# Attention with transposed rows in batches of eight key blocks, their products with V one batch behind

## The chip, the cores and the metric

The kernel runs on one core of one Trainium2 chip, in one launch. The metric is the time of that launch in microseconds (us). The kernel before has a median of 4274.78 us over three runs (4272.74 to 4277.41).

## What is computed

The reference is a trunk of two layers over 2048 tokens of width 1024, in float32. Each layer normalises x, projects it, and runs four groups of four heads (64 dims each) in parallel: A stick-breaking attention, B latent attention, C attention over 256 keys chosen by an indexer, D differential attention. The groups' outputs are gated, joined and projected back. Cut to the part that the change touches:

```python
def softmax_attention(q, k, v, scale):        # B; C and D have the same last line
    def block(i, qb, kk, vv):                 # a query tile of 128, all keys up to it
        s = einsum('bqhd,bshd->bhqs', qb, kk) * scale
        p = softmax(where(vis, s, -inf))
        return einsum('bhqs,bshd->bqhd', p, vv)
# D: w = softmax(s1) - lam * softmax(s2), then w @ v
# C: the softmax runs over the chosen keys alone
```

## The kernel before

A layer is worked off in sweeps over 16 query tiles of 128 tokens: `a` (group A and the indexer of C), `h` (latents and gates), `d0` and `d1` (group D, two heads in each), `b`, `c`, `o` (output projection). Query tile i sees nb = i + 1 key blocks of 128.

In D, B and C a tile is split into units, one per head (in C two heads at a time for i < `PAIRED` = 12). A unit has a first part and a second part.

The first part, `att_row` (L826), makes a row: scores of the tile against all keys (TensorE, L837, in PSUM tiles `s`), scaled and copied to a row `rw` in SBUF with the minimum (VectorE, L841 or L843, L846), and their exponentials in place (ScalarE, L847). Rows lie in a ring of `R2` = 30720 bytes per partition (`self.rows`); a row of tile i takes 512 (i + 1) bytes. In D two rows are joined into one with lambda (L1074).

The second part, `att_pv` (L850), multiplies a row by V. TensorE needs the row transposed, so for each group of four key blocks (two blocks of two heads in the paired units of C) it makes four transposes into one PSUM tile `tp` (L283), ScalarE or VectorE copies it to a scratch tile `pt` (L285 or L287), and TensorE multiplies by V into the PSUM tile `y` (L866), even blocks into partitions 0 to 63 and odd ones into 64 to 127. There are two buffers `tp` and three `pt`; the indexer uses `pt` as well (L495, L505). `EV` says how many of the copies go to ScalarE: 0.6 of them in C, all in D, 0.6 in B. A product is one instruction in the program and two records in the trace.

What sets the order: the parts are generators. `drive` (L1338) merges the second part of a unit with the first part of the next unit and with the projections of later tiles (L256, L257, L260) and their transposes (`pj`, L283), each taken in shares of its stated cost (`yield`). The framework then orders every engine's instructions by that priority and by its own estimate of when operands are ready, so TensorE's queue holds the pieces of several units mixed. Each engine works through its queue in order. Behind the two layers stands a branch to a general way that is not taken with these inputs; its instructions are in the built program and not in the trace.

In the rows below, PE is TensorE's matmuls and transposes and PEld its weight loads, DVE VectorE, ACT ScalarE, POOL GpSimd.

Of the kernel before, what the change touches and what calls it, by code (L numbers as in the profile page):

```python
# [18 lines left out]
PSUM = bass.MemoryType.PSUM  # L19
# [38 lines left out]
R2 = 30720  # L58


def merge(*gens):
    """Interleaves generators, whose first item is their whole cost and whose others are costs of steps."""
    act = []
    for g in gens:
        if g is None:
            continue
        tot = next(g)
        act.append([0.0, max(tot, 1.0), g])
    while act:
        a = min(act, key=lambda t: t[0] / t[1])  # L70
        try:
            a[0] += next(a[2])
        except StopIteration:
            act.remove(a)
# [15 lines left out]
class Share:  # L90
    """A generator taken in shares of its cost."""
# [16 lines left out]
class Trunk:  # L108
# [53 lines left out]
    def g2(self, shape, dtype=F32):  # L162
        """scratch of the projections, up to 2 KB"""
        return self.wk.tile(shape, dtype, name="g2", bufs=4)

    def pt(self, shape, dtype=F32):
        """scratch of the attention's inner loops, up to 2 KB"""
        return self.wk.tile(shape, dtype, name="pt", bufs=3)

    def o2(self, shape, dtype=F32):  # L170
        """scratch of the attention's results, up to 2 KB"""
        return self.wk.tile(shape, dtype, name="o2", bufs=2)
# [22 lines left out]
    def split(self, hi, lo, raw, eng="pp"):  # L195
        """hi: raw rounded, lo: what that leaves"""
        if eng[0] == "p":
            self.pcopy(hi, raw)
        else:
            self.nc.scalar.copy(hi, raw)  # L200
        if eng[1] == "p":
            self.psub(lo, raw, hi.bitcast(F32))
        else:
            self.nc.vector.tensor_sub(lo, raw, hi.bitcast(F32))  # L204

    def weights(self, W, key, src, pieces, n, kt=KT, first=False):
        """src [kt*128, cols] in DRAM; pieces (column, count) side by side make n columns."""
        nc = self.nc
        w = W[key] = ([], [], n)
        yield kt * 100.0  # L210
        for k in range(kt):
            # the very first ones come all at once, through the memory of the rows
            raw = self.rows.tile([128, n], F32, name="w_raw0") if first else self.wk.tile([128, 512], F32, name="w_raw")
            o = 0
            for c, m in pieces:
                nc.sync.dma_start(raw[:, o:o + m], src[k * 128:(k + 1) * 128, c:c + m])
                o += m
            hi = self.ring.tile([128, n], F32R, name="w_hi")
            lo = self.ring.tile([128, n], F32R, name="w_lo")
            self.split(hi, lo, raw[:, :n], "ad" if k % 3 in WAD or first and k % 3 == 0 else "pp")  # L220
            w[0].append(hi)
            w[1].append(lo)
            yield 100.0
# [4 lines left out]
    def early(self, i, n):  # L228
        """who splits: ScalarE and VectorE while the attention of tile i leaves them time, else GpSimd"""
        return "ad" if FROM <= i < n else "pp"  # L230
# [32 lines left out]
    def rstd(self, who, ss, n, width):  # L263
        """(ss / width + eps) ** -0.5 of [128, n]"""
        nc = self.nc
        r = self.wk.tile([128, 16], F32, name="rs")[:, :n]
        if who in BYACT:
            nc.scalar.activation(r, ss, AF.Ln, bias=self.eps, scale=1.0 / width)
            nc.scalar.activation(r, r, AF.Exp, scale=-0.5)
            return r  # L270
        nc.gpsimd.tensor_scalar(r, ss, 1.0 / width, EPS, op0=OP.mult, op1=OP.add)  # L271
        nc.gpsimd.tensor_tensor(r, r, self.mhalf[:, :n], op=OP.pow)  # L272
        return r

    def transposes(self, dst, srcs, eng="act", tag="pj"):
        """srcs: up to four [128, m] fp32 views; dst [m, len, 128] view."""
# [3 lines left out]
        # sources of rounded results are rounded themselves  # L280
# [3 lines left out]
        if eng == "act":  # L284
            nc.scalar.copy(dst, p[:m, :len(srcs), :])  # L285
        else:
            nc.vector.tensor_copy(dst, p[:m, :len(srcs), :])  # L287

    def piece(self, st, key, i, shape, dtype=F32):
        """the tile of key that holds token tile i, of four each; last but one dim of shape is 4 tiles long"""  # L290
# [5 lines left out]
    def at(self, offset, g):  # L296
        """generator g, its instructions scheduled as if they came offset instructions later"""
# [17 lines left out]
    def a_load(self, l, i, st):  # L315
        """x tile -> normalised, transposed, split"""
# [41 lines left out]
    def functions_a(self):  # L358
        """has ScalarE take the set of functions with both exponential and logarithm"""
        self.nc.scalar.preload_act_table_set("natural_log_exp_and_others")  # L360

    def a_first(self, l, i, st):
# [33 lines left out]
        for r in range(2):  # L396
# [6 lines left out]
            if zr is not None:  # L403
                # what is left of the stick after these blocks is at most exp(X0 - z0)
# [63 lines left out]
    def hilo64(self, u):  # L468
        """u [128, 5, 64]: [hi lo] of the first four, [hi hi] and [lo lo] of the last"""
# [9 lines left out]
    def ci_score(self, l, i, st, tied=True):  # L479
        """scores of tile i into a row buffer"""  # L480
# [3 lines left out]
        # the general search takes two more rows  # L484
# [3 lines left out]
        for c0 in range(0, n, 512):  # L488
            w = min(512, n - c0)
            # equal scores of zero rank by their index  # L490
# [25 lines left out]
    def ci_search(self, l, b):  # L516
        """per row of the tiles of b a threshold with 249..256 scores at or above it, then the 256th itself"""
# [17 lines left out]
        def count(dst, th):  # L535
            """number of scores at or above th"""
# [24 lines left out]
        # threshold among the zeros: bracket (-(n + 0.5) TINY, Z) .. (0.5 TINY, P0)  # L561
# [13 lines left out]
        # above zero  # L575
# [9 lines left out]
        # below zero  # L585
# [12 lines left out]
        for it in range(NITER):  # L598
# [16 lines left out]
            # outside the bracket: its middle  # L615
# [8 lines left out]
        # the 256th of each row: 256 - count below the threshold found  # L624
# [64 lines left out]
    def ga_att(self, l, i, st):  # L689
        """stick-breaking of query tile i over every key block"""  # L690
# [54 lines left out]
    def gc_search(self, l, i, st):  # L745
        """the 256 greatest scores of each row, equal ones by lowest index: bit by bit"""
# [14 lines left out]
        for bit in range(30, -1, -1):  # L761
# [4 lines left out]
            # from zero up: keep the bit while 256 are at or above; from zero down: while fewer are above  # L766
# [10 lines left out]
        # indices of the equal ones, 4096 for the others  # L777
# [26 lines left out]
    def flag(self):  # L804
        """0 where every check of the short ways held"""
# [20 lines left out]
    def att_row(self, i, passes, scale, mn, ls, bias=None):  # L826
        """a row of masked, scaled, negated scores and their exponentials"""
# [22 lines left out]
    def att_pv(self, i, rows, v, y, ev):  # L850
        """y[0:64 | 64:128, :] += even | odd key blocks of rows^T; rows: list of [128, n], y: [128, len * 128]"""
# [4 lines left out]
        for j0 in range(0, nb, step):  # L856
            js = range(j0, min(j0 + step, nb))
            pt = self.pt([128, 4, 128])
            self.ev += ev
            self.transposes(pt[:, :len(js) * m, :], [r[:, j * 128:(j + 1) * 128] for j in js for r in rows],  # L860
                            eng="act" if self.ev >= 1 else "dve", tag="tp")
            if self.ev >= 1:
                self.ev -= 1
            for c, j in enumerate(js):
                o = 64 * (j % 2)
                nc.tensor.matmul(y[o:o + 64, :], v(j), pt[:, c * m:(c + 1) * m, :].rearrange("p a b -> p (a b)"),  # L866
                                 start=(j < 2), stop=(j >= nb - 2), skip_group_check=True)
            yield (109.0 + 125.0) * m * len(js)

    def att_out(self, i, y, nu):  # L870
        """y [128, nu * 128] (dims of even | odd blocks, queries) -> [128 queries, nu, 64] in PSUM"""
# [9 lines left out]
    def norm_out(self, i, y, ls, col):  # L881
        """four heads' results over their sums, to columns col of scratch"""
# [129 lines left out]
    def rope_gain(self, gq, gk, d):  # L1012
        """[128, (q k), (cos sin), d]: gains as the two products of the rotation meet them"""
# [9 lines left out]
    def tables(self, i, d, g):  # L1023
        """cosines and signed sines of token tile i times the gains of q and k: [128, (q k), (cos sin), d]"""
# [8 lines left out]
    def rope(self, u, w, p, tab, nq, nk, h):  # L1033
        """u = p cos + swapped p sin of nq heads of q and nk of k, with their tables"""
# [67 lines left out]
    def lambdas(self, l):  # L1102
        """-lam and the sub-layer norm's gain times (1 - lam_init)"""
# [18 lines left out]
    def start_h(self, l, st):  # L1122
        """latents of B"""
# [36 lines left out]
    def gates(self, i, h, w, col, tag):  # L1160
        """pre-activations of the gates from column col on"""
# [22 lines left out]
    def proj_b(self, l, i, st):  # L1184
# [40 lines left out]
        # q: [hi hi] [lo lo], k: [hi lo]; rotary part q: [hi hi lo], k: [hi lo hi]  # L1225
# [19 lines left out]
    def prep_b(self, l, i, st):  # L1245
# [4 lines left out]
        # heads 0 1: hi hi lo lo, heads 2 3 the same  # L1250
# [87 lines left out]
    def drive(self, sweeps):  # L1338
        """sweeps: (start, prep, units, l, st); tiles one after another, their projections two tiles ahead"""
# [119 lines left out]
```

## Time and profile before

| what | value |
| --- | --- |
| runs, median (lowest to highest) | 4274.78 us (4272.74 to 4277.41) |
| the profiled execution, first to last instruction | 4276.6 us |
| busy: PE, PEld, DVE, ACT, POOL | 3937.6, 3249.9, 2906.3, 2371.9, 1650.7 us |
| D, layer 0 (both halves) | 670 to 1285 us of the span |
| B, layer 0 | 1285 to 1650 us |
| C, layer 0 | 1650 to 1915 us |
| D, B, C of layer 1 | 2790 to 3405, 3405 to 3770, 3770 to 4035 us |

The profiled execution's time is its span; it lies 1.8 us above the median of the runs. Matmuls are pipelined and their ends are modelled, so that two in a row can overlap in the rows: how long a piece of work holds the engine is read from one start to the next. In the list of waits, "issue" stands for idle time that nothing in the profile released.

### The profile page before, as it was taken

How to read it: one execution, taken by the hardware profiler on the slowest of the kernel's cores; microseconds unless marked ns; L12 is line 12 of the kernel's file. 1: busy time of each engine (PE TensorE's matmuls, PEld its weight loads, DVE VectorE, ACT ScalarE, POOL GpSimd, SP SyncE). 2: the span in 40 equal slices, each digit the busy share in tenths (PEclk: the TensorE clock that was granted, in tenths of full speed). 3: DMA queues.
4: the chain of work that ended last, by engine and by line, in shares of the span. 5: the costliest groups of instructions: out<-in, count | busy, mean ns of one | idle time of the engine just before them, and what ended most of it. 6: DMA issues, size and time to landing. Idle time of an engine off the chain costs nothing.

```text
span 4276.6 us, 75274 instructions
## 1 busy us (share of the span) xinstructions
PE 3937.6 (92%) x25833; PEld 3249.9 (76%) x25833; DVE 2906.3 (68%) x10326; ACT 2371.9 (55%) x4846; POOL 1650.7 (39%) x2350
## 2 busy tenths in 40 slices
PE   6999996899988999999989999979999889999999
PEld 6877786777866777777878787867788667777777
DVE  3798788787875655663337988887968766555622
ACT  3656677465665545454126667765666655554621
POOL 2333423665664433420033343337747544344100
PEclk9999997899988999999999999979999899999999
DMA  3222531121110002114522225311211100021144
GB/s 104 80 77 84 175 112 58 50 59 52 50 35 26 19 23 68 50 44 139 167 88 81 81 91 172 114 54 48 61 53 49 36 22 18 26 74 46 59 138 139
DMA packets 204842, 312.60 MB, mean 73 GB/s; under 512 B 63777, under 2 KB 147873, under 8 KB 203937
## 3 DMA queue, kind: packets, MB, share of 16 engines
q1 hardware_dynamic: 204448, 307.69, 22.7%
q8 instruction: 206, 3.38, 0.3%
q14 instruction: 188, 1.53, 0.1%
HBM read 211.89 MB, written 95.72 MB: 72 GB/s over the span
## 4 chain that ended last, share of the span: by engine, by line
PE 57%; DVE 20%; ACT 6%; POOL 6%; DMA 5%; issue 5%; SPq 0%; DVEq 0%; ACTq 0%; POOLq 0%
PE y L866 9%; PE s L837 8%; PE tp L283 7%; PE pj L256 7%; PE pj L257 6%; PE pj L260 6%; PE s L256 3%; PE s L257 3%; PE s L260 3%; ACT junk L538 2%; DVE sc L506 2%; DVE rw L843 2%; PE pj L283 2%; DMA w_raw<-w_in 2%; DVE rw L841 2%
## 5 line engine op out<-in xcount | busy, mean ns | idle before, releaser
L256 PE MATMUL pj<-w_hi,h_hi 128*128 128x384 f32 (+4 forms) x2560 | 880.2, 352 | 51.5 <-POOL w_hi L193 22.9
L257 PE MATMUL pj<-w_lo,h_hi 128*128 128x384 f32 (+4 forms) x2560 | 863.9, 345 | 8.0 <-DVE w_lo L204 4.0
L847 ACT ACTIVATE rw<-rw,at_mn 128x896 f32<-128x896 f32 (+15 forms) x512 | 615.7, 1204 | 173.1 <-DVE at_mn L846 148.2
L285 ACT COPY pt<-tp 128x512 f32<-128x512 f32 (+3 forms) x689 | 358.1, 529 | 467.8 <-PE tp L283 390.3
L256 PEld LDWEIGHTS pj<-w_hi,h_hi 128*128 128x128 f32 x2560 | 505.7, 198 | 88.9 <-POOL w_hi L193 26.0
L283 PE MATMUL tp<-ident,rw 128*128 128x128 f32 x3264 | 540.4, 287 | 34.4 <-DVE rw L1074 20.3
L257 PEld LDWEIGHTS pj<-w_lo,h_hi 128*128 128x128 f32 x2560 | 505.3, 197 | 32.4 <-DVE w_lo L204 6.6
L260 PE MATMUL pj<-w_hi,h_lo 128*128 128x384 f32 (+4 forms) x2560 | 523.4, 338 | 0.0
L283 PEld LDWEIGHTS tp<-ident,rw 128*128 128x128 f32 x3264 | 365.4, 143 | 172.2 <-issue 117.5
L843 DVE TENSOR_SCALAR_CACHE_REDUCE rw<-s 128x512 f32<-128x512 f32 x576 | 383.0, 684 | 108.2 <-PE s L837 73.7
L260 PEld LDWEIGHTS pj<-w_hi,h_lo 128*128 128x128 f32 x2560 | 434.1, 190 | 25.7 <-issue 10.8
L271 POOL TENSOR_SCALAR rs<-ss 128x2 f32<-128x2 f32 (+4 forms) x224 | 61.7, 276 | 802.8 <-DVE ss L987 202.7
L538 ACT ACTIVATE junk<-sg,st_T 128x1152 int8<-128x1152 f32 (+4 forms) x224 | 293.9, 1312 | 83.9 <-DVE st_T L622 56.9
L272 POOL TENSOR_TENSOR rs<-rs,mhalf 128x8 f32<-128x8 f32 (+5 forms) x256 | 317.0, 1239 | 16.9
L287 DVE COPY pt<-tp 128x512 f32<-128x512 f32 (+3 forms) x247 | 152.9, 619 | 197.6 <-PE tp L283 163.5
L837 PE MATMUL s<-dk,qa 96*128 96x512 f32 (+3 forms) x640 | 233.5, 424 | 43.9 <-DVE rw L843 22.3
L187 POOL TENSOR_TENSOR h_lo<-x4a,h_hi 128x1024 fp32r<-128x1024 f32 x103 | 255.5, 2480 | 39.4 <-PE pj L260 22.8
L193 POOL TENSOR_SCALAR hl<-g 128x256 fp32r<-128x256 f32 (+1 forms) x384 | 151.2, 408 | 286.9 <-DVE g L452 61.3
L837 PE MATMUL s<-bk,qa 128*128 128x512 f32 (+6 forms) x960 | 257.8, 394 | 1.2 <-DVE at_mn L841 0.7
L283 PE MATMUL pj<-identr,hl 128*128 128x128 f32 (+1 forms) x1280 | 174.6, 258 | 74.1 <-POOL hl L187 47.9
L193 POOL TENSOR_SCALAR h_hi<-x4a 128x1024 fp32r<-128x1024 f32 x103 | 115.2, 1119 | 319.8 <-PE pj L257 156.1
L841 DVE CUSTOM_DVE_ANT_0 rw<-s,maskR 128x128 f32<-128x128 f32 (+3 forms) x400 | 187.7, 478 | 56.7 <-PE s L837 55.5
(267 smaller groups left out, 8731.5 us busy)
## 6 DMA issues: line engine op xcount, KB each, us to landing
x4a<-hT SPq DMA_DIRECT2D x128, 512.0 KB, 3.5
x4a<-x SPq DMA_DIRECT2D x32, 512.0 KB, 3.5
hT<-x4a SPq DMA_DIRECT2D x32, 512.0 KB, 2.6
x4a<-y SPq DMA_DIRECT2D x32, 512.0 KB, 3.5
x4b<-gate SPq DMA_DIRECT2D x32, 512.0 KB, 3.6
x4c<-x SPq DMA_DIRECT2D x32, 512.0 KB, 4.1
y<-o SPq DMA_DIRECT2D x96, 128.0 KB, 2.1
w_raw<-w_in SPq DMA_DIRECT2D x48, 192.0 KB, 2.6
```

The costliest lines, as they stand in the source:

```text
L256: nc.tensor.matmul(p[:, :n], hi[:, k, :], whi[k], start=(k == 0), stop=False)
L257: nc.tensor.matmul(p[:, :n], hi[:, k, :], wlo[k], start=False, stop=False)
L260: nc.tensor.matmul(p[:, :n], lo[:, k, :], whi[k], start=False, stop=(k == kt - 1))
L272: nc.gpsimd.tensor_tensor(r, r, self.mhalf[:, :n], op=OP.pow)
L283: nc.tensor.transpose(p[:m, j, :].bitcast(dst.dtype), s.bitcast(dst.dtype), ident)
L285: nc.scalar.copy(dst, p[:m, :len(srcs), :])
L538: nc.scalar.activation(self.junk[:, :ns[g]], Sg[g], AF.Sign, bias=th[:, g:g + 1], scale=-1.0, accum_out=dst[:, g:g + 1])
L837: nc.tensor.matmul(p[:, :w], x, y, start=(k == 0), stop=(k == len(ops) - 1))
L841: nc.vector.tensor_tensor_reduce(o, p[:, :w], b, -scale, 3.0e38, OP.add, OP.min, m)
L843: nc.vector.tensor_scalar(o, p[:, :w], -scale, None, op0=OP.mult, op1=OP.min, accum_out=m)
L847: nc.scalar.activation(rw, rw, AF.Exp, bias=mn, scale=-1.0, accum_out=ls)
L866: nc.tensor.matmul(y[o:o + 64, :], v(j), pt[:, c * m:(c + 1) * m, :].rearrange("p a b -> p (a b)"), start=(j < 2), stop=(j >= nb - 2), ski ...
```

## The change

`att_pv` takes two groups at a time as a batch: up to eight transposes and two copies. The products of a batch are made by a new function, `pv_batch`, after the transposes of the next batch have been recorded. The first product of a batch is made to wait for the last copy of the batch. The scratch tiles `pt` get a fourth buffer, and the ring of the rows becomes 128 bytes smaller. `transposes` now returns its copy instruction. The other lines of the difference take comments out, so that lines are numbered anew: products are L880, scores L836, transposes stay L283.

```diff
-R2 = 30720
+R2 = 30592
...
     def pt(self, shape, dtype=F32):
-        return self.wk.tile(shape, dtype, name="pt", bufs=3)
+        return self.wk.tile(shape, dtype, name="pt", bufs=4)
...
         if eng == "act":
-            nc.scalar.copy(dst, p[:m, :len(srcs), :])
-        else:
-            nc.vector.tensor_copy(dst, p[:m, :len(srcs), :])
+            return nc.scalar.copy(dst, p[:m, :len(srcs), :])
+        return nc.vector.tensor_copy(dst, p[:m, :len(srcs), :])
...
     def att_pv(self, i, rows, v, y, ev):
         nc = self.nc
         nb = i + 1
         m = len(rows)
         step = 4 // m
-        for j0 in range(0, nb, step):
-            js = range(j0, min(j0 + step, nb))
-            pt = self.pt([128, 4, 128])
-            self.ev += ev
-            self.transposes(pt[:, :len(js) * m, :], [r[:, j * 128:(j + 1) * 128] for j in js for r in rows],
-                            eng="act" if self.ev >= 1 else "dve", tag="tp")
-            if self.ev >= 1:
-                self.ev -= 1
+        groups = [range(j0, min(j0 + step, nb)) for j0 in range(0, nb, step)]
+        before = None
+        for g in range(0, len(groups), 2):
+            pts = []
+            for js in groups[g:g + 2]:
+                pt = self.pt([128, 4, 128])
+                self.ev += ev
+                last = self.transposes(pt[:, :len(js) * m, :], [r[:, j * 128:(j + 1) * 128] for j in js for r in rows],
+                                       eng="act" if self.ev >= 1 else "dve", tag="tp")
+                if self.ev >= 1:
+                    self.ev -= 1
+                pts.append((js, pt))
+            yield 109.0 * m * sum(len(js) for js, _ in pts)
+            if before is not None:
+                yield self.pv_batch(before, m, nb, v, y)
+            before = pts, last
+        yield self.pv_batch(before, m, nb, v, y)
+
+    def pv_batch(self, batch, m, nb, v, y):
+
+        pts, last = batch
+        first, n = True, 0
+        for js, pt in pts:
             for c, j in enumerate(js):
                 o = 64 * (j % 2)
-                nc.tensor.matmul(y[o:o + 64, :], v(j), pt[:, c * m:(c + 1) * m, :].rearrange("p a b -> p (a b)"),
-                                 start=(j < 2), stop=(j >= nb - 2), skip_group_check=True)
-            yield (109.0 + 125.0) * m * len(js)
+                x = self.nc.tensor.matmul(y[o:o + 64, :], v(j), pt[:, c * m:(c + 1) * m, :].rearrange("p a b -> p (a b)"),
+                                          start=(j < 2), stop=(j >= nb - 2), skip_group_check=True)
+                if first:
+                    self.tc.add_manual_dep(x.ins, last.ins.name,
+                                           mybir.DependencyInfo(mybir.DependencyClass.Sync, mybir.DependencyReason.DATA),
+                                           reason="one run of products")
+                first = False
+                n += m
+        return 125.0 * n
```

How the built order changes is shown at three places; the numbers tell the buffers apart.

First, TensorE in B of layer 0, query tile 12 (13 key blocks, so groups of 4, 4, 4 and 1 blocks per head): `tp` are transposes of a row, `y` products of a `pt` with V. Before:

```order
L283 MATMUL tp_19071<-ident_199,rw_18930 128x128 x4
L837 MATMUL s_19278<-bk_17135,qa_18595 128x512 x3
L866 MATMUL y_18937<-pt_19044,bv_15295 64x128 x4
L283 MATMUL tp_19087<-ident_199,rw_18930 128x128 x4
L866 MATMUL y_18937<-pt_19070,bv_16180 64x128 x4
L283 MATMUL tp_19103<-ident_199,rw_18930 128x128
L866 MATMUL y_18937<-pt_19086,bv_17035 64x128 x4
L283 MATMUL tp_19123<-ident_199,rw_19037 128x128 x4
L866 MATMUL y_18937<-pt_19102,bv_18166 64x128
```

The same head with the change:

```order
L283 MATMUL tp_19074<-ident_199,rw_18930 128x128 x4
L283 MATMUL tp_19081<-ident_199,rw_18930 128x128
L880 MATMUL y_18937<-pt_19044,bv_15295 64x128 x4
L880 MATMUL y_18937<-pt_19051,bv_16180 64x128 x4
L836 MATMUL s_19289<-bk_17137,qa_18598 128x512 x3
L283 MATMUL tp_19123<-ident_199,rw_19037 128x128 x4
L283 MATMUL pj_18966<-identr_201,hl_18878 128x128 x2
L283 MATMUL pj_18972<-identr_201,hl_18879 128x128 x2
L283 MATMUL pj_18966<-identr_201,hl_18878 128x128 x2
L880 MATMUL y_18937<-pt_19073,bv_17036 64x128 x4
L880 MATMUL y_18937<-pt_19080,bv_18163 64x128
```

Products of two groups now follow each other, and two runs of products stand where four stood.

Second, TensorE in B of layer 0, query tile 5 (6 key blocks: one batch of 4 and 2 blocks per head). Before:

```order
L283 MATMUL tp_16877<-ident_199,rw_16773 128x128 x4
L283 MATMUL tp_16902<-ident_199,rw_16773 128x128 x2
L866 MATMUL y_16875<-pt_16876,bv_15295 64x128 x4
L283 MATMUL tp_16941<-ident_199,rw_16868 128x128 x4
L866 MATMUL y_16875<-pt_16901,bv_16180 64x128 x2
L283 MATMUL tp_16961<-ident_199,rw_16868 128x128 x2
L283 MATMUL pj_16652<-identr_201,hl_16596 128x128 x2
L866 MATMUL y_16875<-pt_16940,bv_15295 64x128 x4
```

With the change:

```order
L283 MATMUL tp_16877<-ident_199,rw_16773 128x128 x4
L283 MATMUL tp_16884<-ident_199,rw_16773 128x128 x2
L283 MATMUL tp_16941<-ident_199,rw_16868 128x128 x4
L880 MATMUL y_16875<-pt_16876,bv_15295 64x128 x4
L880 MATMUL y_16875<-pt_16883,bv_16180 64x128 x2
L283 MATMUL tp_16948<-ident_199,rw_16868 128x128 x2
L283 MATMUL pj_16652<-identr_201,hl_16592 128x128 x2
```

The first transposes of the next head (`rw_16868`) now stand ahead of the products of this head, which are one run.

Third, TensorE in the second half of D, layer 0, query tile 12, second head of the half. Before:

```order
L283 MATMUL tp_14926<-ident_199,rw_14867 128x128 x4
L866 MATMUL y_14810<-pt_14897,dv_14137 64x128
L283 MATMUL tp_14974<-ident_199,rw_14867 128x128 x4
L837 MATMUL s_14988<-dk_14289,qa_14550 128x256
L837 MATMUL s_14998<-dk_11641,qa_14550 128x512
L866 MATMUL y_14810<-pt_14925,dv_11475 64x128 x4
L283 MATMUL tp_15006<-ident_199,rw_14867 128x128 x4
L837 MATMUL s_15016<-dk_12543,qa_14550 128x512
L866 MATMUL y_14810<-pt_14973,dv_12426 64x128 x4
```

With the change:

```order
L283 MATMUL tp_14926<-ident_199,rw_14878 128x128 x4
L283 MATMUL tp_14933<-ident_199,rw_14878 128x128 x4
L836 MATMUL s_15029<-dk_13342,qa_14553 128x512
L283 MATMUL tp_14974<-ident_199,rw_14878 128x128 x4
L836 MATMUL s_15037<-dk_14292,qa_14553 128x256
L283 MATMUL tp_14981<-ident_199,rw_14878 128x128
L880 MATMUL y_14810<-pt_14925,dv_11490 64x128 x4
L880 MATMUL y_14810<-pt_14932,dv_12424 64x128 x4
L836 MATMUL s_15083<-dk_11644,qa_14553 128x512
L880 MATMUL y_14810<-pt_14973,dv_13204 64x128 x4
```

All transposes of the head now stand ahead of its first product.

## Rows read from the trace of the kernel before

**Rows 1.** The page, busy us of each engine, share of the span, instructions

```profile
PE 3937.6 (92%) x25833; PEld 3249.9 (76%) x25833; DVE 2906.3 (68%) x10326; ACT 2371.9 (55%) x4846; POOL 1650.7 (39%) x2350
```

**Rows 2.** D, D, B, C of layer 0: length, busy PE, PEld, DVE, ACT, POOL; clock

```profile
670.00:980.00 310.00, 266.35 (x1832) 230.89 (x1832) 258.23 (x932) 186.03 (x388) 183.33 (x246) 0.88 0.18 54
980.00:1285.00 305.00, 276.89 (x2054) 232.12 (x2050) 233.38 (x814) 193.56 (x439) 179.60 (x256) 0.94 0.16 46
1285.00:1650.00 365.00, 349.87 (x2700) 277.71 (x2701) 224.68 (x774) 197.42 (x407) 141.25 (x253) 0.97 0.09 26
1650.00:1915.00 265.00, 255.97 (x1743) 190.79 (x1741) 157.12 (x504) 134.19 (x243) 97.51 (x129) 0.99 0.17 52
```

**Rows 3.** Chain of waits by line, of 670:1285 (D), 1285:1650 (B), 1650:1915 (C)

```profile
by line: PE pj L256 10.2%; PE pj L257 9.4%; PE pj L260 8.3%; PE y L866 8.3%; issue 6.7%; PE tp L283 6.4%; PE s L837 5.8%; DVE rw L843 5.6%; DVE rw L1074 3.1%; POOL rs L272 2.6%; DVE rw L841 2.6%; POOL h_lo L187 2.4%; PE pj L283 2.4%; POOL h
...
by line: PE s L837 24.6%; PE y L866 20.6%; PE tp L283 16.6%; PE pj L283 4.7%; PE pj L256 3.9%; PE pj L257 3.4%; PE y L878 3.3%; PE pj L260 3.3%; DVE rw L841 2.1%; POOL rs L272 1.9%; DVE g L1217 1.4%; DVE g L1215 1.4%; DVE rw L843 1.2%; DVE 
...
by line: PE y L866 18.3%; PE tp L283 18.0%; PE s L837 15.3%; PE pj L256 6.6%; PE pj L257 6.2%; PE pj L260 6.1%; DVE rw L841 5.0%; issue 2.9%; DMA w_raw<-w_out 2.7%; PE y L878 2.2%; PE pj L283 1.9%; ACT rw L847 1.7%; DVE h_lo L204 1.6%; DMA 
```

**Rows 4.** Timeline of PE in B: start, busy us, line, out<-in, tile, shape, xcount

```profile
1394.75 1.04 PE L283 MATMUL tp<-ident,rw 128*128 128x128 f32 x8
...
1400.37 0.66 PE L283 MATMUL tp<-ident,rw 128*128 128x128 f32 x4
1400.96 0.66 PE L866 MATMUL y<-pt,bv 128*64 128x128 f32 x8
...
1543.01 0.66 PE L866 MATMUL y<-pt,bv 128*64 128x128 f32 x8
1543.60 0.33 PE L283 MATMUL tp<-ident,rw 128*128 128x128 f32 x1
...
1549.51 0.60 PE L283 MATMUL tp<-ident,rw 128*128 128x128 f32 x4
...
1553.31 1.53 PE L866 MATMUL y<-pt,bv 128*64 128x128 f32 x24
1554.77 1.67 PE L837 MATMUL s<-bk,qa 128*128 128x512 f32 x6
```

**Rows 5.** Timeline of PEld in B, in brackets the idle time before and its releaser

```profile
1536.89 0.42 PEld L283 LDWEIGHTS tp<-ident,rw 128*128 128x128 f32 x4 [0.17 <-issue]
1537.28 1.60 PEld L837 LDWEIGHTS s<-bk,qa 128*128 128x128 f32 x9
...
1553.31 1.29 PEld L866 LDWEIGHTS y<-pt,bv 128*64 128x64 f32 x24 [0.17 <-issue]
```

**Rows 6.** Busy time by stretch, tile 15 of B in layer 0, columns as in rows 2

```profile
1617.20:1649.80 32.60, 32.13 (x283) 27.30 (x284) 20.77 (x68) 20.94 (x49) 10.59 (x17) 1.00 0.19 59
```

**Rows 7.** The page's groups: busy us, mean ns of one, idle before, releaser

```profile
L847 ACT ACTIVATE rw<-rw,at_mn 128x896 f32<-128x896 f32 (+15 forms) x512 | 615.7, 1204 | 173.1 <-DVE at_mn L846 148.2
L285 ACT COPY pt<-tp 128x512 f32<-128x512 f32 (+3 forms) x689 | 358.1, 529 | 467.8 <-PE tp L283 390.3
```

**Rows 8.** Who waited for whom, PEld: us in total, times, longest us

```profile
PEld tp L283 <- issue: 117.5, 509, 3.1
PEld y L866 <- issue: 83.8, 325, 1.6
...
PEld y L866 <- ACT pt L285: 24.9, 46, 2.4
...
PEld y L866 <- DVE pt L287: 15.7, 24, 2.2
...
PEld tp L283 <- ACT pt L285: 11.6, 25, 1.0
```

**Rows 9.** Who waited for whom, in the indexer

```profile
ACT pt L505 <- DVE sc L506: 39.8, 31, 2.9
...
PEld s L502 <- ACT pt L505: 11.4, 19, 2.6
```

**Rows 10.** Instructions on the tile `pt`: durations min/median/max ns

```profile
L866 PE MATMUL y<-pt,bv x2176: 272/273/476, 1288.1 to 3769.6; 128*64 128x128 f32 x198
```

## Prediction

> **What bounds the kernel now.** I read four views, from coarse to fine. The engine totals name the candidate: TensorE is busy 92% of the span, no other engine over 68% [rows 1]. The table by stretches says where that is true. In latent attention (B, layer 0, 1285 to 1650 us) TensorE is busy 349.87 of 365 us, in attention over chosen keys (C, 1650 to 1915) 255.97 of 265, but in the two halves of differential attention (D, 670 to 1285) 266.35 of 310 and 276.89 of 305, with VectorE at 258.23 in the first [rows 2]; the second layer looks alike. The chain of waits confirms it: of what ended last, the TensorE lines shown add up to 80% in B, 75% in C and 51% in D [rows 3]. So a microsecond of TensorE's queue is worth nearly one in B and C, about half of one in D.
>
> The timeline shows what such a microsecond is made of. In B transposes and products with V alternate: four transposes from 1400.37, then four products (8 records) from 1400.96; four products from 1543.01, then a transpose from 1543.60. Each group of four holds the engine 0.59 us [rows 4]. The timeline of weight loads shows 0.17 us without any load where products follow transposes or transposes follow products, released by nothing but "issue" [rows 5].
>
> **What one change of kind costs.** Inside a run the same work is cheaper. Twelve products (24 records) begin at 1553.31 and the next work at 1554.77: 1.46 us. Four take 0.59. Eight more therefore cost 0.87, or 0.435 per four, and four that stand apart cost 0.15 more. For transposes, eight are busy 1.04 us and four that do not follow products 0.60, so four more cost 0.44; four behind products take 0.59, again 0.15 more [rows 4]. A run of products that disappears takes one change on either side with it: 0.15 + 0.15 = **0.30 us**.
>
> **The change, term by term.** Transposes, copies, products and rows are the same in number, so only order, waits and buffers count.
>
> Counting TensorE's order as built, up to the branch to the general way, runs of products fall from 690 to 469: in B from 257 to 174 (83 fewer), in C from 213 to 150 (63), in D from 220 to 145 (75). At 0.30 us this is 25, 19 and 22 us, together 66. Runs of transposes fall only from 831 to 771; I count nothing for these, since transposes followed by scores show no such gap (from 1536.89 to 1537.28 in the loads [rows 5]).
>
> What of it shows: in B between 0.80 (chain) and 0.96 (busy share), I take 0.90, being nearest to the later tiles, where the engine is busy 32.13 of 32.60 us [rows 6]: 22.5. In C between 0.75 and 0.97, 0.85: 16. In D between 0.51 and 0.88, 0.60, nearer the chain because the first half is VectorE's almost as much: 13. Sum 51.5; the lower ends give 46, the upper ends 62.
>
> The new wait: the first product of a batch waits for the last copy of that batch. A copy takes 529 ns on ScalarE in the mean [rows 7]. TensorE's weight loads wait now for copies before products 24.9 + 15.7 us, before transposes 11.6 us [rows 8]. There are 936 groups and will be 544 batches, each with one wait in place of one per group. Products lie a batch further back, so that wait can shrink, by 42% of 40.6, or 17 us. But a batch takes both PSUM buffers of the transposes, so the next batch's second group must find two copies done: that wait can grow, and queued behind it stand scores and projections. Nothing in the trace shows how much. Ends: a gain of 17, and a cost of twice the present 11.6, or 23. I take a cost of 8, above the middle, because the two-buffer limit is certain and the shrinking is not. That leaves **43 us**.
>
> The fourth scratch buffer also serves the indexer. Its weight loads wait 11.4 us for ScalarE there, and ScalarE 39.8 for VectorE [rows 9]. Bounds 0 and 11; I take 0, since VectorE, the last in that chain, does no less. The row buffer loses 128 bytes: four rows of tile 14 (7680 bytes each) filled it exactly, and now three fit. I cost that at nothing: in tile 15 the rows (8192 bytes) already fit only three times, and there TensorE has 0.47 us idle in 32.6 [rows 6]. Its cover is the scores of the next row; without it, each of the eight sweeps could lose one exponential (1.20 us mean, [rows 7]), 10 us. The DMA queues get the same transfers and lie off this path.
>
> The sum is made against the profiled execution, 4276.6 us, of which 43 is 1.0%; the median of the three runs is 1.8 below, so the forecast is 4274.8 - 43 = **4232 us**.
>
> **Rivals.**
> 1. *The copies become the wait in D: slower.* D puts every copy on ScalarE. Its two-group batches number 128 (16 per pass over the 16 tiles and head, eight such passes). If TensorE has no other work while the second copy runs, each loses one copy, 529 ns mean [rows 7]: 68 us. D's gain is then gone, B and C keep 38.5 less 8: 4275 - 30 + 68 = 4313. It decides from about 60 batches on. For it: ScalarE also has exponentials of 1.20 us in the same queue. Against: ScalarE is idle 467.8 us ahead of these copies, 390.3 of them waiting for the transposes, so it mostly waits for TensorE and not the reverse [rows 7]; and in the built order scores, projections or the next unit's transposes usually stand between.
> 2. *The rows decide: no change.* If what TensorE saves turns into waiting for scores, minima and exponentials, D returns its 22, B and C half of theirs (22 left), and the waits for copies cost 20: 4273. For it: D's chain, half of which is not TensorE. Against: TensorE's busy share in B and C [rows 2].
> 3. *Loads overlap only across row groups: no change.* In the rows, loads inside a run do overlap the work: 24 loads are done in 1.29 us, one per 0.054, while one product takes 272 ns [rows 5, 10]; so a run is cheaper than its parts, and this rival gives 0 saved, 4275. The Trainium skill ("TensorE: Matmul & The Clock Gate", Part 3, "The mechanism") says that a weight load overlaps a matmul in flight only when the row groups differ. By that rule products and transposes, which use all 128 rows alike, would pay for every load in any order, and merging would save nothing; this case's trace, with 0.054 us per load, does not agree inside a run.
>
> **How the numbers follow.** Forecast 0.72. Its own range is 4205 to 4262: the upper ends without a cost and half of the 17 save 70; the lower ends less costs of 23 and 10 save 13. Still larger gains, if waits for copies vanish too, 0.04. Rival 1 0.11, rival 2 0.09, rival 3 0.04. The three runs lie within 0.11%, so 0.2%, 8.5 us, is what a measurement can tell from no change: faster is 0.76, the same 0.13, slower 0.11. The range 4196 to 4283 takes in the no-change cases and part of the larger gains, and leaves out rival 1 and little else.
>
> **What would show it.** Right: "issue" ahead of products and transposes falls from 201 us [rows 8] by some third (690 to 469 runs); the timeline of B shows products in runs of 16 records; B becomes shorter by about 11 us per layer, C by 8, D by 6 in both halves together. Wrong: B keeps its 365 us while the runs are longer (rival 3, or rows); D grows and weight loads wait for ScalarE's copies well over 24.9 us (rival 1); TensorE's wait for minima or exponentials grows (rival 2). If the row buffer matters, tile 14 grows and tile 15 does not.

## The result and the profile after

The changed kernel takes 4312.70 us (median of four runs, 4308.32 to 4322.13), the kernel before 4275.40 in the same comparison: ratio 1.0084, interval 1.0068 to 1.0100. It is 37 us slower where 43 us less were forecast. The time is the one that rival 1 gave, but not for rival 1's reason.

The page of the changed kernel, the lines that answer to rows 1 and 7:

```profile
PE 3927.7 (91%) x25833; PEld 3295.1 (76%) x25833; DVE 2904.5 (67%) x10326; ACT 2368.1 (55%) x4846; POOL 1641.3 (38%) x2350
...
L846 ACT ACTIVATE rw<-rw,at_mn 128x896 f32<-128x896 f32 (+15 forms) x512 | 616.1, 1205 | 193.8 <-DVE at_mn L845 166.3
L285 ACT COPY pt<-tp 128x512 f32<-128x512 f32 (+3 forms) x689 | 355.6, 530 | 375.4 <-PE tp L283 344.9
```

The instructions are the same and cost the same. Where the time went is read from stretches that begin and end at the same work: D from its first product to B's first, B from there to C's first, in both layers. The table by stretches of the kernel before (length; busy PE, PEld, DVE, ACT, POOL; granted clock, DMA share, GB/s):

```profile
672.80:1288.10 615.30, 542.19 (x3863) 461.49 (x3862) 492.10 (x1733) 377.54 (x821) 365.98 (x508) 0.91 0.17 49
1288.10:1652.40 364.30, 350.51 (x2712) 278.64 (x2712) 223.41 (x767) 197.33 (x407) 140.55 (x250) 0.97 0.09 27
2797.10:3408.30 611.20, 534.80 (x3887) 455.55 (x3887) 492.50 (x1732) 379.12 (x827) 369.38 (x508) 0.93 0.17 51
3408.30:3772.30 364.00, 350.26 (x2711) 278.20 (x2711) 221.65 (x766) 196.92 (x407) 138.49 (x247) 0.97 0.09 26
```

The same of the changed kernel:

```profile
670.40:1304.50 634.10, 543.70 (x3866) 470.50 (x3865) 500.63 (x1793) 385.95 (x832) 361.81 (x507) 0.90 0.16 48
1304.50:1659.60 355.10, 340.27 (x2732) 282.45 (x2732) 219.89 (x768) 197.09 (x411) 143.15 (x251) 0.97 0.10 29
2813.30:3457.80 644.50, 545.18 (x3864) 469.27 (x3864) 509.16 (x1843) 396.51 (x844) 360.08 (x504) 0.89 0.16 47
3457.80:3813.70 355.90, 341.34 (x2712) 281.61 (x2712) 221.38 (x766) 196.78 (x407) 137.65 (x247) 0.97 0.10 27
```

B is shorter by 9.2 and 8.1 us. D is longer by 18.8 and 33.3 us, and its granted clock is lower. So the merged runs do pay in B, and most of the loss is in D. A further 9 us lie between C's first product in layer 0 and D's first in layer 1 (1144.7 us before, 1153.7 after). From C's first product in layer 1 to the end it is 504 us before and 501 after.

The waits of PEld in the changed kernel, which answer to rows 8 (us in total, times, longest):

```profile
PEld tp L283 <- issue: 71.2, 230, 6.0
PEld y L880 <- issue: 61.7, 269, 0.5
...
PEld tp L283 <- ACT pt L285: 28.1, 46, 2.7
...
PEld y L880 <- DVE pt L286: 13.0, 17, 1.5
...
PEld y L880 <- ACT pt L285: 12.0, 28, 1.0
```

The gaps that end by "issue" ahead of products and transposes fell from 201 to 133 us, by 34%; 68 us for 221 runs fewer is 0.31 us per run, near the price in the prediction. That the two agree is in part chance: this is idle time of the weight loads and not of the products, and one gap in it lasts 6.0 us, far over the 0.17 of a change of kind [rows 5]. The waits of products for ScalarE's copies halved [rows 8], those of transposes for ScalarE's copies grew from 11.6 to 28.1; together they are 36.5 us before and 40.1 after. And in B the runs look as expected; the timeline of PE in the changed kernel:

```profile
1511.40 1.09 PE L880 MATMUL y<-pt,bv 128*64 128x128 f32 x16
1512.43 0.66 PE L283 MATMUL tp<-ident,rw 128*128 128x128 f32 x4
1513.01 0.66 PE L880 MATMUL y<-pt,bv 128*64 128x128 f32 x8
1513.60 0.66 PE L283 MATMUL tp<-ident,rw 128*128 128x128 f32 x4
```

Eight products (16 records) hold the engine 1.03 us, four 0.59: 0.44 for four more, the price forecast.

What grew is TensorE's wait for D's joined rows. Over the whole run, in the kernel before and in the changed kernel:

```profile
PE tp L283 <- DVE rw L1074: 20.3, 21, 2.9
PE tp L283 <- DVE rw L1094: 45.0, 43, 5.7
```

### The profile page after: what moved, and what is told of

It reads as the page before. It is cut to its first block, busy times and chain, and to the rows that moved or that the text cites. A ratio compares the mean times of both kernels' runs of the same rounds, so it can differ in the third digit from the quotient of the medians.

```text
span 4314.7 us, 75241 instructions
## 1 busy us (share of the span) xinstructions
PE 3927.7 (91%) x25833; PEld 3295.1 (76%) x25833; DVE 2904.5 (67%) x10326; ACT 2368.1 (55%) x4846; POOL 1641.3 (38%) x2350
## 4 chain that ended last, share of the span: by engine, by line
PE 38%; DVE 10%; ACT 4%; issue 3%; DMA 3%; POOL 2%; SPq 0%; DVEq 0%; ACTq 0%; POOLq 0%
PE y L880 6%; PE s L836 5%; PE tp L283 5%; PE pj L256 4%; PE pj L257 3%; PE pj L260 3%; PE s L256 3%; PE s L257 3%; PE s L260 2%; ACT junk L537 2%; PE pj L283 1%; DVE sc L505 1%; PE y L898 1%; DMA w_raw<-w_in 1%; DVE rw L842 1%
## 5 line engine op out<-in xcount | busy, mean ns | idle before, releaser
L257 PE MATMUL pj<-w_lo,h_hi 128*128 128x384 f32 (+4 forms) x2560 | 873.3, 349 | 9.2 <-POOL w_lo L187 5.1
L283 PE MATMUL tp<-ident,rw 128*128 128x128 f32 x3264 | 535.2, 288 | 74.7 <-DVE rw L1094 45.0
L283 PEld LDWEIGHTS tp<-ident,rw 128*128 128x128 f32 x3264 | 385.4, 146 | 178.1 <-issue 71.2
L193 POOL TENSOR_SCALAR hl<-g 128x256 fp32r<-128x256 f32 (+1 forms) x384 | 166.6, 448 | 312.5 <-DVE g L451 70.2
L836 PE MATMUL s<-dk,qa 96*128 96x512 f32 (+3 forms) x640 | 237.3, 430 | 35.3 <-DVE at_m L840 11.3
L836 PE MATMUL s<-bk,qa 128*128 128x512 f32 (+6 forms) x960 | 255.0, 392 | 2.8 <-DVE at_mn L840 1.8
L283 PE MATMUL pj<-identr,hl 128*128 128x128 f32 (+1 forms) x1280 | 175.0, 259 | 85.3 <-POOL hl L187 57.1
L283 PEld LDWEIGHTS pj<-identr,hl 128*128 128x128 f32 (+1 forms) x1280 | 137.8, 142 | 122.2 <-POOL hl L187 75.4
```

The costliest lines, as they stand in the source:

```text
L193: self.nc.gpsimd.tensor_scalar(o, a, 1.0, 0.0, op0=OP.mult, op1=OP.add)
L257: nc.tensor.matmul(p[:, :n], hi[:, k, :], wlo[k], start=False, stop=False)
L283: nc.tensor.transpose(p[:m, j, :].bitcast(dst.dtype), s.bitcast(dst.dtype), ident)
L836: nc.tensor.matmul(p[:, :w], x, y, start=(k == 0), stop=(k == len(ops) - 1))
```

## The experiments

My first theory was that batches in D ask for transposes before the joined rows are ready. The rivals were the memory (the fourth scratch buffer, the 128 bytes of the row ring), and that any new order scatters the time. The first four runs take the change apart, each compared with the kernel before on the same chip (4276.42 us).

**D in groups of four, the rest of the change kept.** `att_pv1` is the old function:

```diff
 # units_d
-            yield from self.att_pv(i, [ctx[u]], lambda j: st["dv"]...
+            yield from self.att_pv1(i, [ctx[u]], lambda j: st["dv"]...
```

> The changed kernel, but D makes and multiplies its rows in groups of four as before; B and C keep the batches; the fourth scratch buffer and the smaller row ring stay. Theory (the batches in D are what costs: transposes asked for earlier wait for joined rows, and the clock falls with the waits): the D stretch of both layers goes back from 634 and 645 us to 615 and 611, B keeps 349 and 352, the whole 4313 - 52 = about 4261. Rival (buffers or ring): D stays over 630, the whole 4300 or more. Rival (any new order scatters): anything within 4275 +- 25, with B or C also off by more than 5 us.

4315.91 us, ratio 1.0095 (1.0078 to 1.0112). D stayed at 631 and 653 us. The first theory falls: without batches D is as slow.

**Batches in D alone.** The same exchange in C and B instead of D.

> The batches in D alone; B and C as before; fourth scratch buffer and smaller ring as in the change. Theory: B and C back at 361 us per layer for B, D at 634 and 645, the whole about 4275 + 52 = 4327. Rival (buffers): as slow as the run with buffers alone. Rival (scatter): 4275 +- 25.

4335.63 us, ratio 1.0137 (1.0120 to 1.0154).

**The buffers alone.**

```diff
 # the kernel before
-R2 = 30720
+R2 = 30592
...
-        return self.wk.tile(shape, dtype, name="pt", bufs=3)
+        return self.wk.tile(shape, dtype, name="pt", bufs=4)
```

> The kernel before with the fourth scratch buffer and the smaller row ring, groups of four as before. Theory: 4275 +- 8, D at 615 and 611. Rival (buffers or ring make D slow): D at 630 or more, the whole 4320 or more.

4333.42 us, ratio 1.0132 (1.0115 to 1.0149): the rival's number, and the same as with batches in D. So the change in memory costs 57 us, and with these buffers batches in D are worth nothing either way.

**The row ring alone.** Only the first of these two lines.

> The kernel before with the row ring 128 bytes smaller and nothing else. Theory: 4275 +- 8. Rival (the ring: three rows of tile 14 where four fitted): 4290 or more, with tile 14 and tile 4 of D longer by 5 us or more each. Rival (scatter): a change of 10 us or more in either direction that sits in no one tile.

4318.24 us, ratio 1.0100 (1.0083 to 1.0117). One line, 128 bytes, costs 42 us. The first theory's number (4275) is out. The rival's number came and its sign did not. Read from result to result, tile 14 of D did not grow, and tile 4 grew by 5 us or more in one half of D out of four (24.7 to 50.4 us); there it is long with the larger ring too (47.4, below), which costs nothing.

What these bytes do is seen in the built order. The kernel before and this one have the same order up to tile 14 of the first half of D, layer 0. There it differs first on VectorE, at the score copies of a fourth row of that tile (`at_m_11679`):

```
 L1067 TENSOR_SCALAR d_c<-d_c,d_l_11444,nlam_241 128x1
 L1074 SCALAR_TENSOR_TENSOR rw<-rw,d_c 128x512 x3
-L843 TENSOR_SCALAR rw,at_m_11679<-s 128x512
 L1095 TENSOR_TENSOR rs<-rs,at_rl 128x2
 L1089 RECIPROCAL at_rl<-d_l_11444 128x2
-L843 TENSOR_SCALAR rw,at_m_11679<-s 128x512 x2
 L1097 SCALAR_TENSOR_TENSOR o_11578<-y,rs,gsub_244 128x64 x2
+L843 TENSOR_SCALAR rw,at_m_11679<-s 128x512 x3
```

Four rows of tile 14 are 30720 bytes; in 30592 the fourth waits for a place. Rows of tiles 9 and 11 lose a place as well (five in place of six, four in place of five), and the order at these tiles is the same. With 30464 bytes the built order is the same as with 30592, and with 30848 the same as with 30720: a step, not a slope.

On the chip the cost shows best at the last tile of D in layer 1. The stretch from tile 14's result to tile 15's (L1093), in the kernel before, columns as above:

```profile
3374.50:3397.50 23.00, 19.66 (x153) 16.30 (x151) 14.85 (x61) 15.32 (x47) 15.98 (x25) 0.85 0.13 33
```

In the kernel with the smaller ring alone:

```profile
3396.30:3432.10 35.80, 25.37 (x163) 19.99 (x163) 23.14 (x77) 19.83 (x51) 17.61 (x27) 0.71 0.08 21
```

And in the changed kernel:

```profile
3412.10:3446.80 34.70, 24.04 (x165) 20.06 (x164) 22.74 (x77) 19.73 (x52) 17.34 (x27) 0.75 0.09 22
```

The timeline of PE with the smaller ring alone tells what it waits for, in brackets:

```profile
3403.18 1.08 PE L283 MATMUL tp<-ident,rw 128*128 128x128 f32 x4 [5.72 <-DVE rw L1074]
...
3406.81 1.94 PE L283 MATMUL tp<-ident,rw 128*128 128x128 f32 x8 [1.23 <-DVE rw L1074]
...
3421.03 2.02 PE L283 MATMUL tp<-ident,rw 128*128 128x128 f32 x8 [2.26 <-DVE rw L1074]
```

L1074 is the joining of D's two rows: the transposes stand ready and the row is not. The list of waits has, in the stretch of the kernel before, of the one with the smaller ring, and of the changed kernel, in this order:

```profile
PE tp L283 <- DVE rw L1074: 0.7, 1, 0.7
PE tp L283 <- DVE rw L1074: 9.2, 3, 5.7
PE tp L283 <- DVE rw L1094: 9.9, 3, 5.7
```

The granted clock of the stretch is 0.85 before and 0.71 or 0.75 with the waits: more of the stretch passes at the lower of the two levels (1.2 and 2.4 GHz), so the work between the waits takes longer as well. Four transposes take 1.08 us behind the longest wait (3403.18), and 0.66 later in the same stretch (3425.64).

Read the same way in all four halves of D, tile 15 is longer by 3.3 to 12.8 us with the smaller ring alone, 27 us together, and tile 14 shorter by 0.6 to 4.7, 11 us together. The lost place is in tile 14 and most of the waiting in tile 15; how it gets from one to the other was not traced. The two tiles hold 16 of some 36 us by which D grows.

The new theory: the batches pay as priced, and the ring takes it away. The next three runs test it (before: 4275.67 us).

**The change with the full ring.** Room for the 128 bytes comes from a constant that nothing reads:

```diff
 # the changed kernel
-R2 = 30592
+R2 = 30720
...
-        self.eps = ct([128, 1], F32, name="eps")
-        nc.vector.memset(self.eps, EPS)
```

> The changed kernel with the row ring at 30720 bytes again; room for it is made by leaving out a constant (a column of epsilon) that nothing reads. Ring theory (128 bytes less made D late, and the batches themselves pay): 4313 less the 42 us that the ring alone cost, so 4271 or less, down to the 4232 of the prediction if nothing else costs; D back under 620 us in both layers, B at 349 to 356. Rival (batches cost in D whatever the ring): D stays over 630, the whole 4300 or more.

4267.34 us, ratio 0.9974 (0.9964 to 0.9985): 45 us less than the changed kernel, and now faster than before, but far from 4232. D is 626 and 620 us, not under 620 in both layers as expected; B is 354 and 358.

**A larger ring in the kernel before** (`R2 = 31744`).

> The kernel before with a row ring of 31744 bytes, 1024 more. Ring theory (what counts is that rows of sizes that divide 30720 still fit): 4275 +- 8 or a little faster. Rival (scatter: 30720 was a lucky order and any other loses): 4300 or more, with waits spread over other tiles.

4274.68 us, ratio 0.9997 (0.9988 to 1.0006). More room is worth nothing; 30720 was no lucky order but the last size that fits. D in layer 1 is 628 us here in place of 611, which other stretches make up for, so the length of one stretch is not yet a price.

**The fourth scratch buffer in the kernel before, full ring** (without the unread constant).

> The kernel before with the fourth scratch buffer and the full ring (without the unread constant), groups of four. Ring theory: 4275 +- 10, since the fourth buffer has nothing to do in groups of four. Rival (the fourth buffer itself costs, as the 15 us between the two earlier runs suggest): 4290.

4299.80 us, ratio 1.0049 (1.0034 to 1.0064). The buffer itself costs 24 us in groups of four: the rival's side, and I had costed it at nothing.

Between this kernel and the change with the full ring only the batches differ, with their lag and their wait: 4300 to 4267, 676 runs of products to 472. The next four runs ask what in the batches pays (before: 4273.05 us).

**Batches without the lag, three scratch buffers, full ring.** The products of a batch are recorded right behind its own transposes:

```diff
 # the changed kernel with R2 = 30720 and bufs=3
-            if before is not None:
-                yield self.pv_batch(before, m, nb, v, y)
-            before = pts, last
-        yield self.pv_batch(before, m, nb, v, y)
+            yield self.pv_batch((pts, last), m, nb, v, y)
```

> Batches of eight, but their products recorded right behind their own transposes, with three scratch buffers and the ring of 30720 bytes as in the kernel before: the runs of products without the two costs in memory (498 runs of products against 690, 192 fewer). Theory (runs pay about 0.15 to 0.30 us each, the ring and the fourth buffer are what cost): 4275 - 30 to 55 = 4220 to 4245. Rival (without the lag products wait for copies): weight loads of products wait for copies 60 us or more, the whole 4275 or more.

4258.59 us, ratio 0.9960 (0.9948 to 0.9972). Faster, though by 14 us where 30 to 55 were expected: 0.08 us per run.

**The same with four scratch buffers**, full ring.

> The same with four scratch buffers and the full ring (478 runs). Theory that the fourth buffer by itself costs: 15 to 24 us slower than the run with three. Theory that it costs nothing: the same within 8. Against the run with the lag and full ring (4267) it tells what the lag is worth: the lag pays if this is over 4275.

4244.41 us, ratio 0.9923 (0.9907 to 0.9939), the best of all kernels here and faster than both. Here the fourth buffer gains 14 us, where it cost 24 in groups of four: the buffer has no price of its own.

**Without the added wait**, lag and full ring kept: the lines with `add_manual_dep` are taken out.

> The changed kernel with the full ring, without the added wait for the batch's last copy (the built order then has 662 runs of products instead of 472). Theory (the gain is in the runs): near 4300, as the kernel before with a fourth buffer; B back at 361 us. Rival (the added wait costs): faster than 4267.

4295.65 us, ratio 1.0057 (1.0040 to 1.0075), as in groups of four with these buffers. Without the wait the scheduler mixes other work into the products (662 runs), and the gain is gone: the wait that I had booked as a cost is what makes most of the runs. It is a cost all the same: without it TensorE is idle 342 us in place of 372, but busy 3951 in place of 3901 (the page's busy time, and the span less that).

**D in groups of four, full ring.**

> The changed kernel with the full ring, D in groups of four, B and C in batches (530 runs, 58 fewer saved in D). If batches pay in D too: 8 to 17 us slower than 4267. If what they save in D is returned by later rows: 4267 +- 6. If they cost in D: 4255 or less.

4267.57 us, ratio 0.9989 (0.9978 to 0.9999), level with the 4267.34 of batches everywhere, though it has 58 runs more. By its median what batches save in D is returned there. The ratios (0.9989 here, 0.9974 with batches everywhere) differ by 6 us and their intervals overlap, so a small gain in D is not excluded.

Last, whether ring and lag cost by themselves (before: 4272.87 us).

**Batches without the lag, the ring of 30592 bytes**, four scratch buffers.

> The changed kernel (four scratch buffers, ring of 30592 bytes) with the products recorded right behind their own transposes. If the ring costs by itself, whatever the order of products: 4244 + 33 to 48 = 4277 to 4292. If the lag costs by itself: 20 to 28 us faster than the changed kernel, 4285 to 4293. If either was a matter of one order by chance: outside both, over 4300 or under 4265.

4291.00 us, ratio 1.0046 (1.0025 to 1.0068), inside both expected ranges: the ring costs 47, the lag 22.

The ring's price stands in five pairs: 4276 to 4318 (42), 4300 to 4333 (34), 4267 to 4313 (45), 4268 to 4316 (48), 4244 to 4291 (47). The first pair differs in the ring alone; in the other four the kernel with the full ring also leaves out the unread constant. The lag's price stands in two, 4244 to 4267 (23) and 4291 to 4313 (22). The medians come from several comparisons, whose medians of the kernel before lie between 4272.9 and 4276.4; taken against its own, the ring costs 33 to 47 and the lag 19 to 20.

The pages tell what the ring's price is made of. Their first lines, of the smaller ring alone, of the change with the full ring, and of batches without the lag with four buffers and the full ring (the spans are 4313.9, 4272.9 and 4245.3 us):

```profile
PE 3957.6 (92%) x25833; PEld 3259.2 (76%) x25833; DVE 2909.1 (67%) x10326; ACT 2374.2 (55%) x4844; POOL 1649.2 (38%) x2350
PE 3901.0 (91%) x25833; PEld 3281.3 (77%) x25833; DVE 2891.3 (68%) x10325; ACT 2363.3 (55%) x4846; POOL 1633.4 (38%) x2350
PE 3883.2 (91%) x25833; PEld 3257.9 (77%) x25833; DVE 2895.6 (68%) x10325; ACT 2367.2 (56%) x4846; POOL 1634.2 (38%) x2350
```

TensorE's idle time is the span less its busy time: 339 us in the kernel before, 356 with the smaller ring alone, 372 in the change with the full ring, 387 in the changed kernel. In the five pairs the smaller ring adds 15 to 19 us of idle time, and 16 to 35 us of busy time for the same 25833 instructions. By stretches, D of both layers takes 28 to 39 us of the price. Another 4 to 16 lie between C's first product in layer 0 and D's first in layer 1, where the ring also serves the next layer's indexer (L485, L522); that stretch was not taken apart.

## Why the prediction was wrong

From before (4273.1 in that comparison) to after the steps are, with the medians in us: batches without the lag, -14 (4258.6); a fourth buffer under them, -14 (4244.4); the lag, +23 (4267.3); the ring, +45 (4312.7).

- *The step that failed* is the sentence on the row ring: "I cost that at nothing", with 10 us as its upper end. The arithmetic was right (three rows of tile 14 instead of four) and the price was not. I judged it from tile 15 of B, where each unit needs one row [rows 6]. In D a unit needs two rows that are joined before the first transpose, D was the sweep with the least cover by my own reading [rows 2, 3], and I looked at no tile of D. Measured: 34 to 48 us. TensorE's wait for joined rows rose with it in all five pairs, by 9 to 24 us over the run (20.3 to 31.6 with the smaller ring alone, 21.3 to 45.0 in the change). The sign that I gave for it, tile 14 growing and tile 15 not, was wrong too: tile 15 of the last half of D grew by 12 to 13 us, and tile 14 became shorter by 2 to 4.
- *What made it larger than its waits* is a term that I left out: the clock. It is 0.957 over the run before and 0.952 with the smaller ring alone, 0.953 and 0.947 for the change with the full and the smaller ring. A mean that is lower by 0.005 to 0.006 of full speed takes 21 to 26 us of full-speed time out of 4300. TensorE's busy time grew by 20.0 and 26.7 us in these two pairs, and in the other three it stays within 4 us of what the mean clock gives (falls of 0.003, 0.009 and 0.006; 15.6, 35.0 and 25.8 us more busy time). So between a third and a bit over half of the ring's price is idle time, and the rest agrees with work at the lower clock. No run changes the clock by itself.
- *The lag* was to shrink the waits for copies, with 8 us as net cost. It costs 19 to 23. With the full ring, weight loads of products wait for ScalarE's copies 15.1 us with the lag and 23.7 without, those of transposes 32.1 and 23.0. So the shrinking and the two-buffer limit that I named both came, and cancel. TensorE is idle 10 us longer with the lag and busy 18 longer, at a mean clock of 0.953 against 0.958, which is worth 21 by the same working. Which waits make the idle time was not found.
- *The fourth buffer*, forecast at 0, measured +24, +15 (4318 to 4333) and -14. It moves the order of everything, and its sign depends on what else is there. Why stays open.
- *Right:* the price of a run in the timeline of B, and that products in longer runs are cheaper. In B 11 us per layer were forecast, 9.2 and 8.1 came. In C 8 per layer were forecast; in layer 1, with what follows, 3 came. In D the 13 us did not come, as rival 2 said for D, and it was for rows that TensorE waited longer.
- *The saving*, 51.5 us for 221 runs, is no single number. Where only the batches differ it is 32 us for 204 runs with the lag (4300 to 4267), and 55 us for 198 without it (4300 to 4244); with three buffers and no lag it is 14 us for 192. From the kernel before to the best one TensorE's busy time fell by 54 us at the same mean clock (0.957 and 0.958) and its idle time grew by 23: the work became cheaper about as priced, and part of it came back as waiting, which the forecast had no term for. In D the share on the path, 0.6, was too large: the medians give about 0 there.
- *Rival 1* gave 4313 and the kernel takes 4312.7, by chance: the waits for ScalarE's copies are 4 us longer in all and not 68, and D in groups of four was not faster. *Rival 3* is out, since four products cost 0.44 us inside a run and 0.59 apart. By the rule of the Trainium skill ("TensorE: Matmul & The Clock Gate", Part 3, "The mechanism") that stood beside it they would have stayed as dear; the timeline of B after the change, 0.44 us for four more products inside a run, does not agree.

## What to carry to other kernels

Divide every buffer that a change shrinks by the sizes that live in it, and where a quotient passes a whole number, price the lost place in the stage with the least slack and the longest chain ahead of use, not in the stage that is easiest to read. Here 128 bytes of 30720 cost more than the merged runs of products returned (33 to 47 us against 29 in the best kernel). A reordering that pays should then be tried without its extra buffers and its lag, one at a time: the best kernel here keeps the runs, the added wait and the fourth buffer, has the full ring, and leaves the lag out.

## What was not expected of the hardware

Waits of TensorE went with a cost beyond their length. In the last tile of D, 9.2 us of waits for the joined row, in place of 0.7, stand in a stretch that is 12.8 us longer than before; its granted clock is 0.71 in place of 0.85, TensorE is busy 25.37 us in place of 19.66, and the longest single wait there is 5.7 us. Over whole runs each of the five pairs adds 15 to 19 us of idle time and 16 to 35 us of busy time, and the mean clock falls by 0.003 to 0.009. Between kernels that differ in more than the ring, the mean clock alone does not tell which is slower: it is 0.950 at 4333 us (the buffers alone) and 0.947 at 4313 (the change).
